# Ten raw weight buffers and five low-part buffers in a two-layer decoder trunk, with another landing time in its planner

## The chip, the cores and the metric

The kernel runs on one core of one Trainium2 chip. The metric is the device time of one execution in microseconds (us); of several executions the median is given. The core has five engines that run side by side, each with its own queue of instructions: TensorE (PE; its weight loads are the row PEld), VectorE (DVE), ScalarE (ACT), GpSimd (POOL) and SyncE (SP), which here issues most of the DMA transfers. Sixteen DMA engines carry the transfers.

## The reference

The kernel computes a decoder trunk of two layers for 256 tokens of width 1024, all in float32. Each layer adds a half-step SwiGLU feed-forward part (FFN, inner width 2816), a mixer, a second FFN and a gated embedding (PLE). The mixer of layer 0 is a chunked mLSTM, that of layer 1 a differential attention over keys and values that are computed once after layer 0.

```python
def swiglu(x, w_in, w_out):
    gate, up = jnp.split(x @ w_in, 2, axis=-1)
    return (jax.nn.silu(gate) * up) @ w_out

for layer in range(DEPTH):                       # DEPTH = 2
    g = norm_g[layer]
    h = swiglu(rms_norm(x, g[0]), w_ffn_in[layer, 0], w_ffn_out[layer, 0])
    x = x + 0.5 * rms_norm(h, g[1])
    h = rms_norm(x, g[2])
    if layer < N_A_LAYERS:                       # layer 0
        h = mlstm_mixer(h, mlstm_w_in[layer], mlstm_b_gates[layer],
                        mlstm_head_norm[layer], mlstm_w_out[layer])
    else:                                        # layer 1
        h = diff_attention(h, k_sh, v_sh, diff_w_q[j], diff_lambda[j],
                           diff_subln[j], diff_w_out[j], lam_init)
    x = x + rms_norm(h, g[3])
    h = swiglu(rms_norm(x, g[4]), w_ffn_in[layer, 1], w_ffn_out[layer, 1])
    x = x + 0.5 * rms_norm(h, g[5])
    gate = jax.nn.sigmoid(rms_norm(x, g[6]) @ w_ple_gate[layer])
    x = x + rms_norm((p[layer] @ w_ple_proj[layer]) * gate, g[7])
    if layer == N_A_LAYERS - 1:
        k_sh, v_sh = shared_kv(x, kv_norm, w_kv)
```

## The kernel before

**Matmuls in three parts.** A float32 product is made of three matmuls of a rounded type (fp32r): each operand is split into a high part and a low part, and high·high, high·low and low·high are added up in PSUM (`mm3`). For activations these are the tiles `xh`/`xl` and `hh`/`hl`, for weights `whi`/`wlo`. Since every weight is used for only 256 tokens, the weights stream through the core once, a piece of 128x2048 (1 MB) at a time.

**The way of a weight piece** (`weight`, line 482, or `load` and `parts` inside `block_pair`): SP issues a transfer into a raw buffer `wraw`; ACT copies it, rounded, to `whi`; DVE subtracts (`wraw` - `whi`) into `wlo`; PE reads `whi` and `wlo`. The raw buffer is free when DVE's subtraction is done, the two parts when PE's last matmul with them is done. In halves (x2, 128x1024) the two copies are made where a stage begins or ends. `part` (line 472) hands out one `whi` and one `wlo`.

**FFN.** The inner width is cut into eleven blocks of 256. Most blocks are taken in pairs (`block_pair`, line 717) with seven products of quarters in place of eight; for that, sums of weight pieces are needed, which DVE adds in place in `wraw`, or POOL makes by a transfer that adds to what a raw buffer holds. `stage_out` multiplies the gated hidden block (`hh`/`hl`, after a transpose on PE into `tr`) with the output weights into four accumulators `accO`. Input products go to `accI`.

**Raw buffers hold other things too.** The residual x (two halves of one buffer, `pair`), the gains of the next norm, the normed x for the pairs (`pre` with `kept`), and the mLSTM's and the attention's values are `wraw` tiles for a time. There are 9 raw buffers, 6 `whi` and 6 `wlo` (128x2048, 8 KB for each partition).

**What sets the order.** The program is run twice. The first run only notes every operation (`Notes.add`); then `play` (line 266) simulates the engines with a table of costs, and takes at each step, greedily, the operation that can start first, in the order of the program among equals. It also hands out the buffers: a tile gets the next slot that comes free, in the order in which tiles are created. The second run issues the operations in the order found (line 432, which is therefore the line of nearly all instructions in the profile). Each engine then runs its instructions strictly in that order, and waits where the buffer or the data isn't there. In the simulation a transfer's data counts as there some time after its bytes are through: 180 ns and `LATE` for a plain transfer, 810 ns and `SLACK` for one that adds (in `later`, inside `play`):

```python
def later(q, t):
    t += 810 + SLACK if q.kw.get("accum_op") is not None else 180 + LATE
```

The names that the prediction uses: `wraw`, `whi_Nr`, `wlo_Nr` (N is the slot), `hh`/`hl`, `tr`, `accI`/`accO`, `att` (pieces of 128x512 for transposed x, attention and held sums), `sg` (gated hidden block).

Of the kernel before, what the change touches and what calls it, by code (L numbers as in the profile page):

```python
# [10 lines left out]
F32R = mybir.dt.float32r  # L11
# [5 lines left out]
P = 128  # L17
# [7 lines left out]
PEN = 30  # L25
MARGIN = 300
SLACK = 3000
LATE = 600
LANES = 8
DEPTH = 2  # L30
HA = 4
# [2 lines left out]
BIG = 2.0 ** 100  # L34
GKV = 8
ATT = 8
NRAW = 9
NPART = 6
NX = 7
NSG = 3  # L40
NH = 3
# [18 lines left out]
class Notes:  # L60
# [205 lines left out]
    def play(self, margin):  # L266
# [60 lines left out]
        def later(q, t):  # L327
            t += 810 + SLACK if q.kw.get("accum_op") is not None else 180 + LATE
            if t > q.end:
                q.end = t  # L330
                for u in q.users:
                    if u.start is None and u.after[q]:
                        u.ready = max(u.ready, t)
                for v in freed.get(q, ()):
                    given[v] = max(given[v], t)
# [99 lines left out]
def trunk(nc, a):  # L435
    def T(shape, tag, bufs, dt=F32):
        return nc.tile("sb", shape, tag, bufs, dt)
# [32 lines left out]
        nc.vector.scalar_tensor_tensor(dst_lo, src, gc, dst_hi.bitcast(F32), op0=ALU.mult, op1=ALU.subtract)  # L470

    def part():
        return T([P, 2048], "whi", NPART, F32R), T([P, 2048], "wlo", NPART, F32R)


    def pair(*shape):
        b = T([P, 2, *shape], "wraw", NRAW)
        return [b[:, i] for i in range(2)]
# [3 lines left out]
    def weight(src, n=1, m=1, between=None):  # L482
        raw = T([P, 2048], "wraw", NRAW)
        hi, lo = part()
        w = 2048 // n
        was, nc.is_urgent = nc.is_urgent, False
        for i in range(n):
            if between and i in between:
                between[i]()
            c = slice(i * w, (i + 1) * w)  # L490
            nc.sync.dma_start(raw[:, c], src[:, c])
            for i2 in range(m):
                c2 = slice(i * w + i2 * w // m, i * w + (i2 + 1) * w // m)
                split(hi[:, c2], lo[:, c2], raw[:, c2])
        nc.is_urgent = was
        return hi, lo
# [28 lines left out]

    xT = T([P, KD, NT, P], "wraw", NRAW)

# [81 lines left out]
    def quarter_parts():  # L609
        return T([P, 4, P], "xh", NX, F32R), T([P, 4, P], "xl", NX, F32R)  # L610

# [43 lines left out]
    def parked(tiles):  # L655
# [4 lines left out]
        def back():  # L660
            b = T([P, 2, D], "wraw", NRAW)
            nc.sync.dma_start(b, home)
            return [b[:, i].rearrange("p (a b) -> p a b", b=v.shape[2]) for i, v in enumerate(tiles)]
# [53 lines left out]
    def block_pair(xts, xf, src, src2, use, end=False, between=None, nxt=None, t3=None):  # L717
        def load(src, plus=None):
            raw = T([P, 2048], "wraw", NRAW)
            nc.sync.dma_start(raw, src)  # L720
            if plus is not None:
                nc.gpsimd.dma_start(raw, plus, accum_op=ALU.add)
            return raw

        def parts(raw):
            p_ = part()
            split(*p_, raw)
            return p_
# [196 lines left out]
    def ple(l, xts, rs, epilogue):  # L925
        gbc, hg = load_gbc(a["norm_g"][l, 7])
        pT = T([P, 2, S], "att", ATT)
        nc.sync.dma_start(pT, a["pT"][l])
        php = T([P, 2, 2, S], "whi", NPART, F32R)
        ph, pl = php[:, 0], php[:, 1]  # L930
# [572 lines left out]
```

## Time and profile before

| | before |
|---|---|
| time, median of 3 runs | 1009.94 us (1007.89 to 1010.15) |
| profiled execution, time | 1006.51 us |
| profiled execution, span | 1004.7 us |
| granted TensorE clock | 0.999 |
| ACT busy | 697.9 us (69%) |
| POOL busy | 88.6 us (9%) |
| DMA | 274.68 MB, mean 273 GB/s |

The trace runs through the stages one after the other, by the weights that SP loads: first FFN of layer 0 from the start (its last weights at 145 us), mLSTM (weights from 149 to 259), second FFN (262 to 436), PLE and the shared keys and values (444 to 485), first FFN of layer 1 (485 to 665), differential attention (667 to 741), last FFN (741 to 930) and the last PLE (937 to the end). The matmuls of a stage come some 10 to 40 us behind its loads. "[3.83 <-DMA wraw]" at the end of a row is the idle time of that engine just before, and what ended it. In the views by windows the counts stand in parentheses. Matmuls overlap, so two rows in succession start 0.23 us apart though one lasts 0.39.

### The profile page before, as it was taken

Reading aid. Unit: us, or ns where it says so; the run is one execution under the profiler, and the core shown is the slowest. Engines: PE = TensorE matmul, PEld = TensorE weight load, DVE = VectorE, ACT = ScalarE, POOL = GpSimd, SP = SyncE. Lnnn points to the kernel's source line nnn. Section 1 sums busy time; section 2 is a strip of 40 time slices with the busy share of each in tenths; the row PEclk is TensorE's granted clock in tenths of the full one; section 3 lists DMA queues with packets and bytes.
Section 4 is the critical chain, followed back from the end, with each engine's and each line's share of the span. In section 5 each row is a group of like instructions: output and inputs, shape, how many; then the busy total and the mean of one; then the engine's idle time right before and its main releaser. Section 6 shows DMA issues by size and latency. Waiting matters only on the chain. (4 is left out here: it accounts for less than half of the span.)

```text
span 1004.7 us, 12418 instructions
## 1 busy us (share of the span) xinstructions
PE 987.2 (98%) x4636; PEld 803.2 (80%) x4636; DVE 893.1 (89%) x909; ACT 697.9 (69%) x924; POOL 88.6 (9%) x126
## 2 busy tenths in 40 slices
PE   9999999999999999999999999999999999999997
PEld 7888888887787788888887788788888887888886
DVE  6977998788999999998899899998985999999983
ACT  8747767577847867595767767676776787767662
POOL 0000000100131000001120000000002300000010
PEclk9999999999999999999999999999999999999999
DMA  9999778765699999966799999965657898998721
GB/s 345 418 333 335 234 245 301 241 191 186 252 292 339 290 337 311 311 252 221 293 280 321 349 335 326 311 248 222 232 216 230 241 330 285 286 306 283 282 84 42
DMA packets 45860, 274.68 MB, mean 273 GB/s; under 512 B 5481, under 2 KB 5865, under 8 KB 16105
## 3 DMA queue, kind: packets, MB, share of 16 engines
q1 hardware_dynamic: 39752, 231.69, 60.1%
q0 software_dynamic: 5760, 41.95, 20.8%
q8 instruction: 36, 0.59, 0.2%
q10 hardware_dynamic: 288, 0.27, 0.1%
q14 instruction: 24, 0.19, 0.0%
HBM read 263.40 MB, written 10.49 MB: 273 GB/s over the span
## 5 line engine op out<-in xcount | busy, mean ns | idle before, releaser
L432 DVE TENSOR_TENSOR wraw<-wraw,wraw 128x2048 f32<-128x2048 f32 x40 | 91.3, 2282 | 0.2
L432 ACT ACTIVATE whi_0r<-wraw 128x2048 fp32r<-128x2048 f32 (+2 forms) x49 | 77.8, 1597 | 11.7 <-DMA wraw<-in_mlstm_in 3.8
L432 ACT ACTIVATE whi_2r<-wraw 128x2048 fp32r<-128x2048 f32 (+1 forms) x48 | 79.4, 1663 | 7.7 <-PE accI L432 3.5
L432 ACT ACTIVATE whi_1r<-wraw 128x2048 fp32r<-128x2048 f32 (+2 forms) x51 | 78.2, 1542 | 7.4 <-PE accO L432 4.1
L432 ACT ACTIVATE whi_5r<-wraw 128x2048 fp32r<-128x2048 f32 (+1 forms) x44 | 71.7, 1641 | 15.6 <-PE accI L432 11.5
L432 ACT ACTIVATE whi_4r<-wraw 128x2048 fp32r<-128x2048 f32 (+1 forms) x45 | 73.7, 1648 | 6.0 <-PE accO L432 2.6
L432 ACT ACTIVATE whi_3r<-wraw 128x2048 fp32r<-128x2048 f32 (+1 forms) x45 | 74.1, 1648 | 4.9 <-DMA wraw<-in_ffn_in 3.3
L432 ACT ACTIVATE att<-accI 128x512 f32<-128x512 f32 x80 | 47.5, 593 | 34.0 <-PE accI L432 33.7
L432 POOL DMA_DIRECT2D wraw<-in_ffn_in x36 | 32.0, 888 | 426.3 <-DMA wraw<-in_ffn_in 363.3
L432 DVE TENSOR_TENSOR wlo_0r<-wraw,whi_2r 128x2048 fp32r<-128x2048 f32 (+1 forms) x25 | 48.3, 1942 | 1.3 <-ACT whi_2r L432 1.3
L432 DVE TENSOR_TENSOR wlo_3r<-wraw,whi_1r 128x2048 fp32r<-128x2048 f32 (+1 forms) x25 | 48.4, 1941 | 1.1 <-ACT whi_1r L432 1.1
L432 DVE TENSOR_TENSOR wlo_2r<-wraw,whi_2r 128x2048 fp32r<-128x2048 f32 (+1 forms) x21 | 43.7, 2080 | 4.6 <-ACT whi_2r L432 4.5
L432 DVE TENSOR_TENSOR wlo_1r<-wraw,whi_1r 128x2048 fp32r<-128x2048 f32 (+2 forms) x26 | 44.4, 1709 | 3.5 <-ACT whi_1r L432 3.4
L432 DVE TENSOR_TENSOR wlo_1r<-wraw,whi_0r 128x2048 fp32r<-128x2048 f32 (+1 forms) x23 | 46.0, 2005 | 0.4 <-ACT whi_0r L432 0.2
L432 DVE TENSOR_TENSOR wlo_0r<-wraw,whi_0r 128x2048 fp32r<-128x2048 f32 (+2 forms) x24 | 44.1, 1839 | 0.8 <-ACT whi_0r L432 0.6
L432 DVE TENSOR_TENSOR wlo_5r<-wraw,whi_4r 128x2048 fp32r<-128x2048 f32 (+1 forms) x23 | 44.0, 1912 | 0.3 <-ACT whi_4r L432 0.3
L432 DVE TENSOR_TENSOR wlo_4r<-wraw,whi_4r 128x2048 fp32r<-128x2048 f32 (+1 forms) x22 | 43.6, 1991 | 0.3 <-ACT whi_4r L432 0.3
L432 POOL TENSOR_TENSOR sm<-sm,mhalf 128x1 f32<-128x1 f32 (+2 forms) x40 | 32.5, 813 | 109.0 <-DVE sm L432 106.5
L432 DVE TENSOR_TENSOR wlo_2r<-wraw,whi_3r 128x2048 fp32r<-128x2048 f32 (+1 forms) x22 | 41.7, 1894 | 0.3 <-ACT whi_3r L432 0.3
L432 DVE TENSOR_TENSOR wlo_4r<-wraw,whi_5r 128x2048 fp32r<-128x2048 f32 (+1 forms) x22 | 41.4, 1894 | 0.0
L432 POOL TENSOR_SCALAR sm<-sm 128x1 f32<-128x1 f32 x32 | 16.9, 527 | 261.8 <-ACT sg L432 261.8
L432 ACT ACTIVATE sg<-accI,sm 128x256 f32<-128x256 f32 x34 | 16.0, 471 | 32.9 <-PE accI L432 24.2
(617 smaller groups left out, 3041.4 us busy)
## 6 DMA issues: line engine op xcount, KB each, us to landing
wraw<-in_ffn_in SPq DMA_DIRECT2D x102, 1024.0 KB, 9.5
wraw<-in_ffn_out SPq DMA_DIRECT2D x44, 1024.0 KB, 9.3
wraw<-in_ffn_in POOLq DMA_DIRECT2D x36, 1024.0 KB, 12.0
wraw<-in_mlstm_in SPq DMA_DIRECT2D x14, 1024.0 KB, 6.9
wraw<-in_ple_gate SPq DMA_DIRECT2D x8, 1024.0 KB, 5.5
wraw<-in_w_kv SPq DMA_DIRECT2D x8, 1024.0 KB, 5.1
home<-wraw SPq DMA_DIRECT2D x28, 256.0 KB, 4.1
wraw<-home SPq DMA_DIRECT2D x14, 512.0 KB, 3.4
```

The costliest lines, as they stand in the source:

```text
L432: getattr(getattr(self.nc, eng), name)(*args, **kw)
```

## The change

One buffer of 8 KB for each partition moves from the low parts to the raw pieces: ten `wraw` and five `wlo` in place of nine and six; `whi` stays at six. The planner takes a plain transfer to land 1000 ns after its bytes are through (beside the 180) in place of 600. The costs of the operations stay, and so does what is computed.

```diff
-LATE = 600
+LATE = 1000
...
-NRAW = 9
+NRAW = 10
 NPART = 6
+NLOW = 5
...
     def part():
-        return T([P, 2048], "whi", NPART, F32R), T([P, 2048], "wlo", NPART, F32R)
+        return T([P, 2048], "whi", NPART, F32R), T([P, 2048], "wlo", NLOW, F32R)
```

Since the planner hands out buffers and picks the order, instructions move on all engines. Three places matter below. In the rows `wraw_3_80` is raw buffer 3; the number behind it only tells tiles of the pools apart and counts differently in the two kernels.

The first place is SP, the loads of the mLSTM's weights. The mLSTM's input weights come in a group of nine and a group of five. Before, these are the last five loads of the first group and the five of the second:

```order
L432 DMA wraw_8_85<-in_mlstm_in 128x2048
L432 DMA wraw_1_78<-in_mlstm_in 128x2048
L432 DMA wraw_0_77<-in_mlstm_in 128x2048
L432 DMA wraw_2_79<-in_mlstm_in 128x2048
L432 DMA wraw_3_80<-in_mlstm_in 128x2048
...
L432 DMA wraw_1_78<-in_mlstm_in 128x2048
L432 DMA wraw_8_85<-in_mlstm_in 128x2048
L432 DMA wraw_3_80<-in_mlstm_in 128x2048
L432 DMA wraw_4_81<-in_mlstm_in 128x2048
L432 DMA wraw_2_79<-in_mlstm_in 128x2048
```

With the change, the same ten loads (left out in both are x going to its home in DRAM and coming back, and two loads of gains):

```order
L433 DMA wraw_2_78<-in_mlstm_in 128x2048
L433 DMA wraw_3_79<-in_mlstm_in 128x2048
L433 DMA wraw_8_84<-in_mlstm_in 128x2048
L433 DMA wraw_6_82<-in_mlstm_in 128x2048
L433 DMA wraw_0_76<-in_mlstm_in 128x2048
...
L433 DMA wraw_8_84<-in_mlstm_in 128x2048
L433 DMA wraw_3_79<-in_mlstm_in 128x2048
L433 DMA wraw_2_78<-in_mlstm_in 128x2048
L433 DMA wraw_0_76<-in_mlstm_in 128x2048
L433 DMA wraw_5_81<-in_mlstm_in 128x2048
```

The third load of the second group, the one at 221.02 us in the trace of before, takes raw buffer 3 before, which the last load of the first group had filled; with the change it takes raw buffer 2, which the first load of the first group had filled, four loads earlier.

The second place is DVE at the end of the differential attention, ahead of the last FFN; `xl_5r<-tr,sub` is a low part of the attention's result, the `sm4` rows are softmax and norm sums. Before (the two halves of the split at 764.68 us in the trace are the third row):

```order
L432 SCALAR_TENSOR_TENSOR xl_5r_118<-tr_0_97,sub_0_164,xh_5r_111 128x512
L432 TENSOR_TENSOR wlo_4r_75<-wraw_0_77,whi_5r_70 128x1024
L432 TENSOR_TENSOR wlo_1r_72<-wraw_4_81,whi_0r_65 128x1024 x2
L432 SCALAR_TENSOR_TENSOR sm4_4_138<-sm4_2_136,sm4_0_134 128x2
L432 TENSOR_TENSOR wraw_7_84<-accO_2_95,sm4_3_137 128x256
L432 SCALAR_TENSOR_TENSOR sm4_9_143<-sm4_8_142,sm4_7_141 128x2
```

With the change, from the same `xl_5r` row on, and then the rows where that piece's split stands now:

```order
L433 SCALAR_TENSOR_TENSOR xl_5r_118<-tr_0_97,sub_0_164,xh_5r_111 128x512
L433 SCALAR_TENSOR_TENSOR sm4_4_138<-sm4_2_136,sm4_0_134 128x2
L433 TENSOR_TENSOR wraw_2_78<-accO_2_95,sm4_3_137 128x256
L433 SCALAR_TENSOR_TENSOR sm4_9_143<-sm4_8_142,sm4_7_141 128x2
...
L433 SCALAR_TENSOR_TENSOR wraw_8_84<-wraw_1_77,sm1_4_160,wraw_8_84 128x512 x2
L433 SCALAR_TENSOR_TENSOR xl_2r_115<-tr_0_97,sub_0_164,xh_2r_108 128x512
L433 TENSOR_TENSOR wlo_2r_73<-wraw_5_81,whi_4r_69 128x1024
L433 TENSOR_TENSOR att_7_105<-tr_0_97,gcol_0_130 128x512
L433 TENSOR_TENSOR att_2_100<-accI_1_91,gcol_0_130 128x512
L433 TENSOR_TENSOR xl_0r_113<-att_7_105,xh_0r_106 128x512
L433 TENSOR_TENSOR xl_4r_117<-att_2_100,xh_4r_110 128x512
L433 TENSOR_TENSOR wlo_2r_73<-wraw_5_81,whi_4r_69 128x1024
```

One split fewer stands ahead of the attention's last sums; the piece whose split was the third row before is split in two halves after x has been updated (the row into `wraw_8_84`), around the first pieces of the next norm, and the splits behind it come one place later each.

The third place is DVE at the first pair of blocks of the FFN that opens layer 1. Before, from the split in halves at 525.22 us on:

```order
L432 TENSOR_TENSOR wlo_4r_75<-wraw_1_78,whi_5r_70 128x1024 x2
L432 TENSOR_TENSOR wlo_3r_74<-wraw_4_81,whi_1r_66 128x2048
L432 COPY wraw_6_83<-tr_0_97 128x4x128
L432 TENSOR_TENSOR xl_5r_118<-att_1_99,xh_5r_111 128x512
L432 TENSOR_TENSOR wraw_4_81<-wraw_4_81,wraw_5_82 128x2048
L432 TENSOR_TENSOR wlo_1r_72<-wraw_3_80,whi_0r_65 128x2048
L432 SCALAR_TENSOR_TENSOR sg_2_128<-accI_1_91,sm1_2_158,sg_2_128 128x256
```

And with the change:

```order
L433 TENSOR_TENSOR wlo_0r_71<-wraw_4_80,whi_1r_66 128x1024
L433 TENSOR_TENSOR xl_5r_118<-att_0_98,xh_5r_111 128x512
L433 TENSOR_TENSOR wlo_0r_71<-wraw_4_80,whi_1r_66 128x1024
L433 COPY wraw_9_85<-tr_0_97 128x4x128
L433 TENSOR_TENSOR wlo_4r_75<-wraw_3_79,whi_2r_67 128x2048
L433 TENSOR_TENSOR wlo_3r_74<-wraw_2_78,whi_4r_69 128x2048
L433 SCALAR_TENSOR_TENSOR sg_0_126<-accI_0_90,sm1_2_158,sg_0_126 128x256
L433 TENSOR_TENSOR wraw_3_79<-wraw_3_79,wraw_8_84 128x2048
```

The two whole splits (128x2048) of the pair's first pieces now follow each other, and the add in place (`wraw<-wraw,wraw`), which stood between them, follows the gating row.

## The prediction, made before the result was known

> **What bounds the kernel now.** I read the head of the page, then the busy time in pieces of 20 us, then the waits of SP, then the timelines of the pieces that fall behind.
>
> ```profile
> span 1004.7 us, 12418 instructions
> PE 987.2 (98%) x4636; PEld 803.2 (80%) x4636; DVE 893.1 (89%) x909; ACT 697.9 (69%) x924; POOL 88.6 (9%) x126
> ```
>
> PE looks busy throughout, but matmuls overlap, so its row hides pauses. Weight loads (PEld) show them better. The columns below are the piece, its length, then busy time (count) of PE, PEld, DVE, ACT and POOL, the clock, the DMA share, GB/s.
>
> ```profile
> 220.00:240.00 20.00, 19.50 (x89) 15.03 (x88) 16.10 (x26) 14.47 (x20) 0.86 (x1) 1.00 0.82 245
> 240.00:260.00 20.00, 19.50 (x92) 15.63 (x91) 18.85 (x26) 18.08 (x32) 3.01 (x1) 1.00 0.42 156
> 300.00:360.00 60.00, 57.67 (x257) 45.38 (x256) 57.86 (x55) 45.72 (x52) 5.78 (x7) 1.00 0.99 327
> 380.00:400.00 20.00, 20.00 (x92) 16.31 (x91) 19.89 (x16) 13.82 (x14) 0.88 (x1) 1.00 1.01 344
> 640.00:660.00 20.00, 19.01 (x86) 14.99 (x85) 17.61 (x16) 11.01 (x12) 0.00 (x0) 1.00 0.73 256
> 840.00:860.00 20.00, 18.48 (x80) 13.76 (x79) 19.10 (x15) 10.30 (x12) 0.86 (x1) 1.00 1.00 348
> ```
>
> The piece at 380 is a full one: 92 matmuls and 16.31 us of loads in 20.00, or 0.816 of the time. Time that PE loses elsewhere is (16.31 of each 20 us, less the loads) / 0.816: 1.57 at 220, 0.83 at 240, 4.4 over 300 to 360, 1.62 at 640, 3.13 at 840. The other pieces lack less each (260, quoted below, as much as 640), so these places hold most of what an order or a buffer can win: 11.6 us of 1004.7.
>
> [...] By PE's row the places above would hold about 6 us, by the loads about twice that; the terms below rest on single stalls instead.
>
> What sets a weight load's time is its buffer:
>
> ```profile
> SPq L432 <- DVE wraw L432: 143.3, 48, 17.1
> SPq L432 <- DVE wlo_1r L432: 111.1, 25, 16.1
> ```
>
> SP waits for DVE to be done with a raw buffer (total, times, longest); a raw buffer is held from the load's issue until DVE has written the low part. So **a tenth raw buffer lets a load be issued one release earlier**, and one low buffer less makes DVE write a low part only when PE is done with the one five back, not six.
>
> **Part 1, the load that mLSTM's end waits for: -2.0.**
>
> ```profile
> 210.99 2.29 DVE L432 TENSOR_TENSOR wlo_2r<-wraw,whi_2r 128x2048 fp32r<-128x2048 f32 x1 [0.28 <-ACT whi_2r L432]
> 218.68 2.27 DVE L432 TENSOR_TENSOR wlo_3r<-wraw,whi_3r 128x2048 fp32r<-128x2048 f32 x1
> 221.02 0.33 SPq L432 DMA_DIRECT2D wraw<-in_mlstm_in  x1
> 233.10 1.92 ACT L432 ACTIVATE whi_0r<-wraw 128x2048 fp32r<-128x2048 f32 x1 [3.83 <-DMA wraw<-in_mlstm_in]
> 235.53 0.69 DVE L432 TENSOR_TENSOR att<-att,att 128x512 f32<-128x512 f32 x1 [3.76 <-ACT att L432]
> ```
>
> The load at 221.02 waits for the split that ends at 218.68 + 2.27 = 220.95. It lands at 233.10; ACT stands for it 3.83 us with the attention work queued behind it, and DVE stands 3.76 behind ACT. In the new order (the first place of the section on the change) this load takes a buffer filled four loads earlier, whose split is the row at 210.99: free at 213.28, or 7.67 us earlier. That exceeds 3.83, even if half is lost in the queue (share 0.82 here). PE loses 1.57 + 0.83 = 2.4 at 220 to 260. Ends: 0 (the head of the next chain is late anyway) and -2.4. I take -2.0: DVE then runs ahead by its 3.76, which is more than the lost 2.4, but some of 240 to 260 lies in mLSTM's own chain of small steps.
>
> **Part 2, the same in the two long FFNs: -1.2 and -0.6.**
>
> ```profile
> 628.08 2.28 DVE L432 TENSOR_TENSOR wlo_2r<-wraw,whi_3r 128x2048 fp32r<-128x2048 f32 x1
> 635.62 2.28 DVE L432 TENSOR_TENSOR wraw<-wraw,wraw 128x2048 f32<-128x2048 f32 x1
> 637.93 0.33 SPq L432 DMA_DIRECT2D wraw<-in_ffn_in  x1
> 648.80 1.92 ACT L432 ACTIVATE whi_3r<-wraw 128x2048 fp32r<-128x2048 f32 x1 [2.14 <-DMA wraw<-in_ffn_in]
> 651.01 0.42 DVE L432 TENSOR_TENSOR hl_2r<-tr,hh_1r 128x256 fp32r<-128x256 f32 x1 [1.64 <-ACT hh_1r L432]
> 651.49 0.44 PE L432 MATMUL tr<-ident,sg 128*128 128x128 f32 x2 [0.99 <-DVE hl_2r L432]
> ```
>
> The load at 637.93 goes out when the add at 635.62 ends (637.90). ACT stands 2.14 for it, ACT's copy hh_1r and DVE's hl_2r come behind it, and PE stands 0.99 for that (1.15 by the matmuls' starts). One release earlier is the split that ends at 628.08 + 2.28 = 630.36: 7.5 us sooner, against 2.14 needed. I take -1.2, with ends 0 and -1.62 (the piece's whole loss).
>
> ```profile
> 820.68 2.29 DVE L432 TENSOR_TENSOR wlo_1r<-wraw,whi_0r 128x2048 fp32r<-128x2048 f32 x1
> 835.68 0.33 SPq L432 DMA_DIRECT2D wraw<-in_ffn_in  x1
> 846.26 1.92 ACT L432 ACTIVATE whi_3r<-wraw 128x2048 fp32r<-128x2048 f32 x1 [0.55 <-DMA wraw<-in_ffn_in]
> 850.68 0.50 PE L432 MATMUL accO<-wlo_5r,hh_1r 128*128 128x512 f32 x1 [1.15 <-DVE wlo_5r L432]
> ```
>
> At 835.68 the earlier release is 820.68 + 2.29 = 822.97, 12.7 us sooner, but ACT waits only 0.55 for this load, and PE's stall of 1.15 is for DVE, which works 19.10 of 20 us here. I take about the 0.55: -0.6, ends 0 and -3.13 (whole piece).
>
> **Part 3, DVE's lead carried on: -1.0.** Over 300 to 360 PE loses 4.4 us where DVE is busy 57.86 of 60.00. DVE's 3.76 idle at 235 becomes lead if its work up to 300 has data early; but the chain of the next norm holds it up (DVE 18.39 of 20 at 260, below), and what it does in advance needs free low buffers. Ends 0 and -3.76; I take the lower third, -1.0, since the piece at 260 shows DVE waiting again.
>
> ```profile
> 260.00:280.00 20.00, 18.71 (x95) 14.99 (x94) 18.39 (x29) 14.84 (x18) 1.92 (x1) 1.00 0.69 256
> ```
>
> **Part 4, one low part fewer: +1.0.** In a stage where PE has plenty prepared, DVE would wait:
>
> ```profile
> 175.14 2.29 DVE L432 TENSOR_TENSOR wlo_3r<-wraw,whi_3r 128x2048 fp32r<-128x2048 f32 x1
> 180.51 0.61 PE L432 MATMUL accO<-wlo_4r,hh_2r 128*128 128x512 f32 x2
> 194.89 0.40 PE L432 MATMUL accI<-wlo_3r,xh_2r 128*128 128x512 f32 x1
> ```
>
> The fifth buffer back is last read at 180.51 + 0.61 = 181.12, so this write moves 5.98 us; its first use at 194.89 leaves 17.45 us, hence 11.5 remain: nothing is lost. Where DVE is the bound, little is prepared, so the fifth buffer is free in time: at 640.42 DVE writes a low part, and the one five back is read last at 638.30.
>
> ```profile
> 638.30 0.39 PE L432 MATMUL accI<-wlo_1r,xh_3r 128*128 128x512 f32 x1
> 640.42 2.28 DVE L432 TENSOR_TENSOR wlo_3r<-wraw,whi_1r 128x2048 fp32r<-128x2048 f32 x1
> ```
>
> The price falls where one regime meets the other, before the last FFN:
>
> ```profile
> 764.68 2.50 DVE L432 TENSOR_TENSOR wlo_1r<-wraw,whi_0r 128x1024 fp32r<-128x1024 f32 x2
> 781.97 0.62 PE L432 MATMUL accO<-wlo_2r,xh_3r 128*128 128x512 f32 x2
> 764.00:784.00 20.00, 20.00 (x117) 17.09 (x115) 9.10 (x17) 10.13 (x30) 4.58 (x7) 1.00 1.01 302
> 784.00:812.00 28.00, 28.00 (x135) 23.09 (x133) 27.36 (x32) 22.17 (x33) 8.22 (x8) 1.00 0.85 242
> 810.17 2.28 DVE L432 TENSOR_TENSOR wlo_3r<-wraw,whi_1r 128x2048 fp32r<-128x2048 f32 x1
> 812.68 0.40 PE L432 MATMUL accI<-wlo_3r,xh_2r 128*128 128x512 f32 x1
> ```
>
> The split at 764.68 (2.50 us) lies in a stretch where DVE works 9.10 of 20.00 us. With five buffers it must wait for the reading that ends at 781.97 + 0.62 = 782.59; the new order (second place) has it behind the norm. From 784 to 812 DVE works 27.36 of 28.00, so 0.64 is free, and at 812.68 PE uses a low part that was ready at 812.45, 0.23 before. Of 2.50, up to 2.50 - 0.64 - 0.23 = 1.6 then reaches PE, if nothing else in the stretch gives way. The stalls of Part 2 at 840 come after it, and a delayed PE has its later low parts more in advance. I take +1.0; ends 0 and +2.5. At the entry to the first FFN of the second layer a split of the same kind moves too (2.4 us, two halves of 1.22):
>
> ```profile
> 485.40 1.22 DVE L432 TENSOR_TENSOR wlo_3r<-wraw,whi_1r 128x1024 fp32r<-128x1024 f32 x1
> 533.09 2.28 DVE L432 TENSOR_TENSOR wlo_1r<-wraw,whi_0r 128x2048 fp32r<-128x2048 f32 x1
> 535.58 0.40 PE L432 MATMUL accI<-wlo_1r,xh_1r 128*128 128x512 f32 x1
> ```
>
> There the part used at 535.58 was ready 0.21 before, but the new order (third place) puts its split ahead of an add of 2.28 us that stood before it; the two cancel, 0 (ends 0 and +2.4).
>
> **LATE** changes only the order: it lets the plan assume 400 ns more for a plain load. Alone it moves few rows that wait, so it has no term; its ends are the -0.6 and +0.6 of a wait such as the 0.55 at 846.26.
>
> **Sum:** -2.0 - 1.2 - 0.6 - 1.0 + 1.0 = -3.8 on the profiled execution's 1006.51, or 1002.7. The median of the runs shown is 1009.94, 3.43 above this execution; the same change on it gives **1006.1**.
>
> **Rivals.**
>
> *The entries cost DVE in full (slower).* The low parts that move from idle stretches, 2.4 us at 485 and 2.5 at 764, all reach PE, because DVE has only 0.64 us free up to the first use 0.23 later, and Parts 1 to 3 give only -1.0 together. +4.9 - 1.0 = +3.9: **1013.8**. It decides when DVE's free time between the norm and 812 is under the 2.50 moved in. For it: 27.36 of 28.00. Against: the order at 535.58 turns the other way, and ACT and DVE wait on landing at both ends.
>
> *An earlier issue lands no earlier (same).* Where the 16 DMA engines are full (share 0.99 over 300 to 360, 1.00 at 840), a load issued earlier only stands longer behind the ones before it. Then only Part 1's load, with share 0.82 and 0.42, gains: -2.0 + 1.0 = -1.0, **1008.9**. For it: those shares. Against: 0.73 at 640. [...]
>
> *DVE's lead is kept (faster by more).* Part 3 at its end: -3.76 in place of -1.0, so -6.6: **1003.4**. Against: the wait at 260.
>
> *The change does nothing*, since LATE is not what the chip does and DVE is the bound: 1009.9.
>
> **How the numbers follow.** The forecast 40%, the entries in full 17%, no earlier landing 22% and nothing 9%, the lead kept 12%. About 0.3% (3.0 us) is what a measurement of this kernel can tell from no change, so 1006.9 to 1012.9 is the same. Of the forecast's 40%, 7 points lie above 1006.9: faster .33 + .12 = .45, same .07 + .22 + .09 = .38, slower .17. The range runs from 1000.5 (the lead kept and Part 2's ends) to 1013.0 (most of the slower rival left out); about 2 in 10 lie outside.
>
> **What would show it.** Right: ACT no longer waits 3.83 for a load near 233, the loads at 220 to 260 rise to about 32.6 together, and ACT's 2.14 before hh_1r near 649 goes. Part 4: DVE busier past 784, with a new stall of PE for a low part between 800 and 840. Wrong: the same waits on landing at a later place, or loads that stay out longer than now, when the three above took 12.1, 10.9 and 10.6 us from issue to the ACT copy.

## The result, and the profile after

| | before | after |
|---|---|---|
| median of 5 runs | 1009.52 us (1007.67 to 1010.15) | 1003.42 us (1003.14 to 1004.18) |
| ratio, 95% interval | | 0.9942 (0.9928 to 0.9956) |
| profiled execution | 1006.51 us, span 1004.7 | 1004.18 us, span 1002.4 |

The change makes the kernel 6.1 us faster where 3.8 were forecast. The two profiled executions, though, differ by only 2.3 us. So there are two questions: where the 2.3 come from, and where the other 3.8 are.

The head of the page after, and the pieces that were read before (length, then busy time of PE, PEld, DVE, ACT and POOL, the clock, the DMA share, GB/s):

```profile
span 1002.4 us, 12436 instructions
PE 988.7 (99%) x4636; PEld 801.8 (80%) x4636; DVE 893.2 (89%) x909; ACT 700.8 (70%) x926; POOL 96.7 (10%) x126
...
220.00:240.00 20.00, 20.00 (x92) 15.50 (x90) 18.94 (x29) 16.95 (x22) 0.00 (x0) 1.00 0.72 204
240.00:260.00 20.00, 19.60 (x94) 16.01 (x92) 18.70 (x24) 17.76 (x26) 3.02 (x1) 1.00 0.57 211
260.00:280.00 20.00, 20.00 (x102) 16.45 (x102) 19.25 (x31) 12.60 (x22) 1.94 (x3) 1.00 0.77 294
300.00:360.00 60.00, 58.41 (x260) 45.69 (x260) 59.66 (x56) 45.24 (x52) 5.26 (x7) 1.00 1.00 336
640.00:660.00 20.00, 20.00 (x93) 16.40 (x93) 19.46 (x17) 14.43 (x15) 0.00 (x0) 1.00 0.70 267
784.00:812.00 28.00, 27.27 (x125) 21.51 (x124) 27.01 (x30) 20.28 (x27) 7.49 (x6) 1.00 0.90 266
800.00:820.00 20.00, 18.86 (x83) 14.52 (x81) 19.97 (x19) 14.45 (x17) 0.95 (x1) 1.00 0.93 296
840.00:860.00 20.00, 19.70 (x86) 15.24 (x85) 19.39 (x16) 13.92 (x14) 0.86 (x1) 1.00 0.96 317
```

The weight loads rise at 220, 240, 640 and 840, where the prediction looked for it: 30.66 to 31.51 from 220 to 260, 14.99 to 16.40 at 640, 13.76 to 15.24 at 840; and at 260, from 14.99 to 16.45. A new gap stands at 800, 14.52 against the 16.29 that the trace of before has there:

```profile
800.00:820.00 20.00, 20.00 (x96) 16.29 (x95) 19.27 (x24) 19.06 (x25) 1.58 (x3) 1.00 0.92 298
```

Since both kernels run the same matmuls on the same data, each one can be matched. The table gives its start in the kernel that the column names less its start in the first profile of before, in us, as the median over the matmuls of 20 us of before's trace from the place named on. The other columns are experiments that follow below, and the second and third profile of before. Between 240 and 280 the new orders move matmuls against one another, by up to 18 us later and 5 us earlier, so the row at 240 tells little there of how far PE is ahead; the readings go by 220 and 280.

| place | after | low part alone | nine in mLSTM | ten in mLSTM only | before, 2nd profile | before, 3rd profile |
|---|---|---|---|---|---|---|
| 220 | +0.5 | +1.1 | +0.3 | +0.4 | +0.5 | -0.3 |
| 240 | -2.6 | +2.3 | -0.5 | -2.6 | +1.2 | +2.5 |
| 280 | -2.3 | +4.8 | +1.9 | -2.3 | +1.2 | +2.3 |
| 320 | -0.8 | +4.8 | +2.0 | -0.6 | +1.2 | +2.3 |
| 340 | -3.8 | +6.3 | +1.9 | -0.5 | +2.8 | +2.3 |
| 360 | -3.1 | +6.3 | +1.7 | +0.9 | +2.8 | +2.3 |
| 420 | -2.2 | +6.4 | +2.5 | +3.0 | +2.8 | +2.3 |
| 520 | -1.6 | +6.5 | +3.0 | +3.4 | +2.9 | +2.8 |
| 560 | -3.0 | +5.0 | +1.7 | +1.9 | +2.9 | +2.9 |
| 620 | -3.2 | +6.8 | +1.4 | +3.8 | +2.9 | +2.8 |
| 640 | -4.5 | +6.4 | +0.2 | +3.3 | +2.9 | +2.8 |
| 800 | -4.0 | +5.3 | +0.6 | +2.5 | +3.2 | +2.7 |
| 820 | -1.7 | +5.3 | +2.9 | +2.5 | +3.2 | +2.7 |
| 860 | -2.8 | +5.0 | +1.8 | +3.8 | +3.2 | +2.9 |
| 980 | -2.0 | +5.4 | +2.6 | +4.3 | +3.3 | +3.0 |

So the schedule gains 2.8 by mLSTM's end (from +0.5 at 220 to -2.3 at 280), 0.8 by 360, 1.4 between 520 and 560, 1.3 at 640 and 1.1 near 850, and gives back 1.5 from 360 to 520, 0.5 from 640 to 800, 2.3 at 800 and 0.8 after 860. The 1.4 at 520 to 560 come with the low part alone as well (+6.5 to +5.0), which has nine raw buffers, so they belong to the new order and not to the tenth buffer. The same caution holds at 640: both columns with nine raw buffers there fall too, from +6.8 to +5.3 and from +3.8 to +2.5 between 620 and 800. That the tenth buffer makes the gain at 640 is therefore not shown.

The load that mLSTM's end waited for, in the timeline of after:

```profile
214.40 0.33 SPq L433 DMA_DIRECT2D wraw<-in_mlstm_in  x1
...
225.41 1.91 ACT L433 ACTIVATE whi_0r<-wraw 128x2048 fp32r<-128x2048 f32 x1
232.95 1.92 ACT L433 ACTIVATE whi_1r<-wraw 128x2048 fp32r<-128x2048 f32 x1 [2.32 <-DMA wraw<-in_mlstm_in]
...
235.38 0.69 DVE L433 TENSOR_TENSOR att<-att,att 128x512 f32<-128x512 f32 x1 [0.92 <-ACT att L433]
```

It goes out at 214.40 in place of 221.02, and ACT copies it at 225.41 without a wait (before: 233.10 after 3.83). ACT now waits 2.32 for the load behind it, but DVE stands only 0.92 of its 3.76, and PE not at all. At 640 the piece that ACT waited for until 648.80 goes out at 630.32 in place of 637.93 and is copied without a wait:

```profile
630.32 0.33 SPq L433 DMA_DIRECT2D wraw<-in_ffn_in  x1
...
642.29 1.90 ACT L433 ACTIVATE whi_0r<-wraw 128x2048 fp32r<-128x2048 f32 x1
```

### The profile page after: what moved, and what is told of

It reads as the page before. It is cut to its first block, busy times and chain, and to the rows that moved or that the text cites. A ratio compares the mean times of both kernels' runs of the same rounds, so it can differ in the third digit from the quotient of the medians.

```text
span 1002.4 us, 12436 instructions
## 1 busy us (share of the span) xinstructions
PE 988.7 (99%) x4636; PEld 801.8 (80%) x4636; DVE 893.2 (89%) x909; ACT 700.8 (70%) x926; POOL 96.7 (10%) x126
## 4 chain that ended last, share of the span: by engine, by line
PE 78%; DVE 6%; ACT 5%; issue 4%; DMA 4%; POOL 2%; SPq 0%; DVEq 0%; POOLq 0%; ACTq 0%
PE accI L433 47%; PE accO L433 28%; PE tr L433 4%; POOL sm L433 2%; ACT sg L433 1%; DMA wraw<-in_ffn_in 1%; DMA wraw<-in_mlstm_in 1%; DVE wlo_4r L433 1%; DVE att L433 1%; DVE wraw L433 1%; DVE wlo_1r L433 1%; DMA wraw<-in_x 1%; DVE wlo_0r L433 1%; DMA wraw<-in_xT 1%; ACT att L433 1%
## 5 line engine op out<-in xcount | busy, mean ns | idle before, releaser
L433 ACT ACTIVATE sg<-accO 128x512 bf16<-128x512 f32 (+2 forms) x46 | 20.2, 444 | 24.5 <-PE accO L433 21.9
L433 ACT ACTIVATE sg<-att,sm 128x256 f32<-128x256 f32 x54 | 26.7, 503 | 14.1 <-DVE att L433 13.7
L433 PEld LDWEIGHTS tr<-ident,sg 128*128 128x128 f32 x176 | 22.0, 140 | 17.1 <-DVE hl_1r L433 3.9
L433 PE MATMUL tr<-ident,sg 128*128 128x128 f32 x176 | 34.7, 279 | 0.2 <-DVE hl_0r L433 0.2
L433 DVE SCALAR_TENSOR_TENSOR wraw<-wraw,sm,wraw 128x512 f32<-128x512 f32 x32 | 22.7, 749 | 12.7 <-POOL sm L433 12.7
L433 DVE TENSOR_TENSOR att<-accI,att 128x512 f32<-128x512 f32 x40 | 27.4, 684 | 2.7 <-PE accI L433 2.4
L433 ACT ACTIVATE sg<-wraw 128x512 bf16<-128x512 f32 x32 | 20.2, 630 | 12.9 <-DVE wraw L433 11.5
L433 ACT ACTIVATE att<-accI,sm 128x512 f32<-128x512 f32 (+1 forms) x22 | 14.8, 671 | 18.6 <-PE accI L433 18.5
L433 ACT ACTIVATE hh_2r<-tr 128x256 fp32r<-128x256 f32 x28 | 10.6, 378 | 23.4 <-PE accO L433 14.9
L433 DVE SCALAR_TENSOR_TENSOR sg<-att,sm,sg 128x256 f32<-128x256 f32 x54 | 25.6, 479 | 1.6 <-ACT sg L433 1.3
## 6 DMA issues: line engine op xcount, KB each, us to landing
wraw<-in_ffn_in POOLq DMA_DIRECT2D x36, 1024.0 KB, 12.1
```

The source lines that it names most:

```text
L433: getattr(getattr(self.nc, eng), name)(*args, **kw)
```

## The experiments

### Which part of the change counts

**LATE alone**, **the buffers alone**, **the low part given up for nothing**, and **a high part given up in place of the low one**:

```diff
 # LATE alone, against before          # buffers alone, against after
-LATE = 600                            -LATE = 1000
+LATE = 1000                           +LATE = 600
 # low part alone, against after       # high part given up, against after
-NRAW = 10                             -  "whi", NPART ... "wlo", NLOW
+NRAW = 9                              +  "whi", NLOW ... "wlo", NPART
```

(With the high part given up, a `whi` tile of the PLE takes `NLOW` as well.)

> Nine raw buffers, six low parts, LATE 1000. Theory (the tenth raw buffer makes the gain, LATE has no term): 1009.5 +-1.5, and ACT's wait of about 3.8 us for the mLSTM load near 233 stays. Rival (the planner's landing time makes the gain by a better order): about 1003.5 to 1005.

> Ten raw buffers, five low parts, LATE 600. Theory: 1003.4 +-1.5, as with the whole change. Rival (LATE makes the gain): about 1009. Rival (any new order moves the time by some us, whatever the buffers): anywhere between 1000 and 1010.

> Nine raw buffers, five low parts, LATE 1000: the low part is given up and nothing is got for it. Theory: the price of the low part without the gain, 1010.5 to 1014 (the last FFN's entry cost PE about 2.4 us in the changed kernel), with the wait of 3.8 us at the mLSTM's load back. Rival (five low parts cost nothing, and the 2.4 us there come from the new order of the pairs): 1009.5 +-1.

> Ten raw buffers, five high and six low parts, LATE 1000: the tenth raw buffer paid for with a high part. Theory (a high part is held longer than its low part, from ACT's copy on, so it is dearer; ACT, ahead of DVE, is held up): 1004 to 1008, with the mLSTM's wait gone. Rival (parts are in plenty, either can go): 1003.4 +-1. Rival (a high part bounds the chain ACT, DVE, PE everywhere): over 1010.

| | median us (runs) | ratio to before, 95% |
|---|---|---|
| before, same chip | 1009.72 (23) | |
| LATE alone | 1009.80 (12) | 1.0007 (0.9995 to 1.0020) |
| buffers alone | 1004.26 (6) | 0.9947 (0.9930 to 0.9963) |
| low part alone | 1010.84 (12) | 1.0005 (0.9990 to 1.0021) |
| high part given up | 1019.94 (6) | 1.0101 (1.0083 to 1.0119) |

The exchange of buffers makes the gain and LATE has none. With nine raw buffers throughout ACT's wait at mLSTM's end is back; the row is that of the kernel with the low part alone:

```profile
235.33 1.91 ACT L433 ACTIVATE whi_0r<-wraw 128x2048 fp32r<-128x2048 f32 x1 [4.94 <-DMA wraw<-in_mlstm_in]
```

Giving up a low part costs nothing that can be measured: 1.0005 against 1.0007 for LATE alone, which has six. Its median, 1010.84, lies at the lower end of the expected 1010.5 to 1014, but its twelve runs go from 1007.08 to 1012.56, so the expected cost of 1 to 4.5 us isn't shown. A high part is another matter: it is claimed earlier, by ACT's copy, and with five of them the kernel is 10 us slower, over the theory's 1004 to 1008 and as the last rival had it. What makes the 10 us was not taken apart; the longest of PE's waits for a single operand there is one for ACT's copy into a high part:

```profile
845.43 0.65 PE L433 MATMUL accI<-whi_4r,xh_2r 128*128 128x512 f32 x1 [2.18 <-ACT whi_4r L433]
```

### Where the tenth raw buffer is needed

One raw buffer is held empty in a part of the program. The code shows the first of two runs; in the second the two calls stand around the first FFN, and again from the mLSTM's end to the end of the last FFN:

```diff
+    def hold():
+        b = T([P, 2048], "wraw", NRAW)
+        nc.gpsimd.memset(b[:, 0:1], 0.0)
+        return b
+    def let_go(b):
+        nc.gpsimd.tensor_tensor(small(), b[:, 0:1], x[0][:, 0:1], op=ALU.add)
...
+    b = hold()
     xts = mlstm(0, xts, rq, kept, pre(2, rs, xfs=xfs))
+    let_go(b)
```

> The changed kernel with one of the ten raw buffers held empty from the mLSTM's first load to x after its first half. Theory (the tenth buffer gains the 3.0 us at mLSTM's end): PE at 245 us stands 0 to +1 us against before in place of -3.0, ACT's wait of about 4 us for the load comes back, and the later places keep their gains: 1004.5 to 1008.5. Rival (the order, not the buffer): -3.0 at 245 stays and the time is 1003.4 +-1.

> The changed kernel with one raw buffer held empty before the mLSTM and from its end to the end of the last FFN: ten in the mLSTM, nine elsewhere, five low parts. Theory: PE at 245 at about -3 against before, no gain at 640 and 850: 1006.5 +-1.5. Rival (the tenth buffer is worth its most in the FFNs, where raw buffers are waited for 143 us in all): 1009 to 1011.

Nine in the mLSTM: 1010.73 us (12 runs), 1.0001 (0.9987 to 1.0015). Ten in the mLSTM only: 1009.50 us (12 runs), 1.0002 (0.9990 to 1.0014). **Either half alone gives back the whole gain.** For the second the rival's range holds; the first lies above both of its ranges. The table of starts shows how. With ten in the mLSTM only, the gain of the mLSTM is there in full (+0.4 at 220, -2.3 at 280), and gone by 420: from 280 to 420 PE falls back 5.3 us. There DVE, with nine raw buffers, stands idle for ACT:

```profile
353.90 0.48 DVE L433 SCALAR_TENSOR_TENSOR sg<-att,sm,sg 128x256 f32<-128x256 f32 x1 [2.46 <-ACT sg L433]
...
388.84 0.88 DVE L433 SCALAR_TENSOR_TENSOR sg<-att,sm,sg 128x256 f32<-128x256 f32 x2 [1.92 <-ACT sg L433]
```

With ten, DVE works 59.66 of 60.00 us from 300 to 360, and the lead is kept. With nine in the mLSTM, the later gains stay (another 1.2 between 620 and 640), but PE has fallen back to +1.9 by 280. It isn't the load's wait that came back: the load goes out late, at 221.28, and yet ACT waits only 0.76 for it where about 4 were expected. The loss comes behind it, in two pauses of PE for DVE, and the piece of 260 to 280 shows a lower clock:

```profile
230.29 1.92 ACT L433 ACTIVATE whi_0r<-wraw 128x2048 fp32r<-128x2048 f32 x1 [0.76 <-DMA wraw<-in_mlstm_in]
...
268.00 0.66 PE L433 MATMUL tr<-ident,wraw 128*128 128x128 f32 x4 [1.08 <-DVE wraw L433]
270.81 0.50 PE L433 MATMUL accI<-wlo_3r,xh_4r 128*128 128x512 f32 x1 [2.14 <-DVE wlo_3r L433]
...
260.00:280.00 20.00, 16.77 (x70) 13.19 (x69) 18.16 (x29) 14.37 (x17) 1.92 (x1) 0.91 0.79 303
```

The same pair of pauses (1.1 and 2.14 us) stands in LATE alone and in the low part alone, near 270, but not in before, which has nine raw buffers and LATE 600. All three plan with LATE 1000 and nine buffers there, so it belongs to that order, and not to a late load. Every change of the buffers changes the order too, and no run here holds the order still: what the tenth buffer gains by the load alone is not separated from what it gains by the order.

The lower clock was the lead to the missing 3.8 us.

### The clock behind a pause

The kernel before was profiled twice more, and the changed one once more.

> The kernel before, unchanged, another profiled execution. Between the two first profiles the spans differ by 2.3 us, the medians by 6.1. Theory (the rest is TensorE's clock: where PE pauses for over about 2 us, the granted clock is 0.5 for some 3.5 us after, as at 274 us in the run with LATE alone; in the first profile of before no pause did it, in most of its executions one to three do): a span of 1006 to 1010 with one to three pieces of 20 us at about 0.91, each behind a pause of PE at 270, 340, 650 or 849, and each worth 1.7 us. Rival (loads land later in most executions than in the first profile): the clock is 1.00 throughout and the span is over 1006 all the same.

> The same again; as for the first look. By the theory the number of pieces below 0.95 orders the spans of the three profiles of before, at about 1.7 us for each.

> The changed kernel, unchanged, a second profiled execution. Clock theory (the changed kernel has no pause of PE long enough): no piece of 20 us under 0.99 between 20 and 980 us, span 1001.5 to 1003. Rival (the first profile of the changed kernel had luck, as the first of before): a piece near 0.91 and a span near 1004.

| execution | span, us | pieces of 20 us below 0.99 from 20 to 980 us |
|---|---|---|
| before, first profile | 1004.7 | none |
| before, second profile | 1008.0 | 0.91 at 340 |
| before, third profile | 1007.7 | 0.94 at 220, 0.97 at 240 (one stretch across both) |
| after, first profile | 1002.4 | none |
| after, second profile | 1001.7 | none |

The first profile of before was its fast end. The spans do stand in the order of the drops of the clock (none, one, one), but 3.0 to 3.3 us apart, where 1.7 for each was expected: the second thing that differs is the rival's, a load that lands later. In the second profile, PE's two waits near 342 are the same as in the first, but here the clock goes to half behind them (pieces of 2 us):

```profile
341.91 0.50 PE L432 MATMUL accI<-whi_1r,xh_1r 128*128 128x512 f32 x1 [1.14 <-ACT whi_1r L432]
343.30 0.50 PE L432 MATMUL accI<-wlo_4r,xh_2r 128*128 128x512 f32 x1 [0.89 <-DVE wlo_4r L432]
...
342.00:344.00 2.00, 1.11 (x4) 0.71 (x5) 2.00 (x3) 2.00 (x3) 0.00 (x0) 0.99 0.23 82
344.00:346.00 2.00, 2.00 (x7) 1.52 (x6) 2.00 (x2) 0.14 (x1) 0.87 (x1) 0.50 0.78 246
346.00:348.00 2.00, 2.00 (x8) 1.58 (x7) 2.00 (x2) 0.29 (x1) 0.00 (x0) 0.66 1.13 315
```

And the first profile of before, at the same waits:

```profile
340.69 0.50 PE L432 MATMUL accI<-whi_1r,xh_1r 128*128 128x512 f32 x1 [1.14 <-ACT whi_1r L432]
342.08 0.50 PE L432 MATMUL accI<-wlo_4r,xh_2r 128*128 128x512 f32 x1 [0.89 <-DVE wlo_4r L432]
...
344.00:346.00 2.00, 2.00 (x10) 1.63 (x10) 2.00 (x2) 1.05 (x2) 0.87 (x1) 1.00 0.90 369
```

Seven matmuls in 2 us in place of ten. The two pieces at 0.50 and 0.66 have lost (0.50 + 0.34) x 2 = 1.7 us, and the column of the second profile jumps by 1.6 there. In the third profile ACT copies the load at mLSTM's end 1.3 us later than in the first (at 234.38, with a wait of 5.43), PE pauses for 2.10 where it paused for 0.50, and the clock drops behind it:

```profile
236.83 0.50 PE L432 MATMUL accI<-whi_4r,xh_4r 128*128 128x512 f32 x1 [2.10 <-ACT att L432]
...
220.00:240.00 20.00, 17.90 (x78) 13.95 (x77) 14.51 (x24) 13.61 (x18) 0.61 (x1) 0.94 0.82 242
240.00:260.00 20.00, 19.60 (x91) 15.75 (x90) 17.99 (x26) 17.27 (x31) 3.01 (x1) 0.97 0.33 109
```

That is a coincidence seen several times, not yet a cause. So four pauses were put into the changed kernel, in its first FFN, where PE is the bound (`last` is what the matmul before wrote, `w` a small tile):

```diff
+            if i in PAUSES:          # ahead of four products' first matmul
+                nc.scalar.activation(w[:, 4:5], last[:, 0:1], AF.Copy)
+                for n in (4, 5, 4, 5):
+                    nc.gpsimd.tensor_scalar(w[:, 9 - n:10 - n], w[:, n:n + 1], w[:, 7:8], None, op0=ALU.add)
+                nc.tensor.matmul(args[0][:, 0:1], ident, w[:, 4:5], start=True, stop=True)
```

> The changed kernel with four pauses of PE put into the first FFN near 41, 58, 75 and 89 us, where low parts lie ready for 9 us and more: ACT reads one column of the product that has just ended, POOL copies it four times (0.53 us each), and one small matmul of PE reads the last copy and holds the next product up. By the rows of those operations a pause is 2.6 to 3.4 us. Clock theory (a pause of over about 2 us is followed by a granted clock of 0.5 for some 3.5 us): pieces of 20 us at about 0.91 behind most of the four, each worth 1.7 us beside the pause itself, so 1003.4 + 10.4 to 13.6 for the pauses + 3.4 to 6.8 for the clock = 1017 to 1024. Rival (the drops that other runs show have another cause and only fall beside pauses): clock 1.00 throughout, 1013.8 to 1017. A pause that is made up later (rival of both) would give under 1013.

1024.09 us (4 runs), 20.7 above the changed kernel and at the upper end of the clock theory's range. The four pauses, and the pieces of 4 us behind the second and the third:

```profile
44.87 0.59 PE L442 MATMUL accI<-mhalf,ident 128*128 128x1 f32 x2 [3.43 <-POOL mhalf L441]
66.84 0.38 PE L442 MATMUL accI<-mhalf,ident 128*128 128x1 f32 x2 [1.83 <-POOL mhalf L441]
87.62 0.38 PE L442 MATMUL accI<-mhalf,ident 128*128 128x1 f32 x2 [1.83 <-POOL mhalf L441]
107.31 0.38 PE L442 MATMUL accI<-mhalf,ident 128*128 128x1 f32 x2 [3.50 <-POOL mhalf L441]
...
64.00:68.00 4.00, 2.17 (x11) 1.54 (x10) 0.48 (x1) 0.54 (x2) 1.13 (x4) 0.99 1.00 268
68.00:72.00 4.00, 4.00 (x14) 3.09 (x13) 0.71 (x2) 0.39 (x2) 0.09 (x1) 0.58 1.00 414
...
84.00:88.00 4.00, 2.17 (x11) 1.51 (x11) 1.03 (x2) 0.54 (x2) 1.23 (x5) 1.00 0.00 0
88.00:92.00 4.00, 4.00 (x13) 3.14 (x13) 0.37 (x1) 0.38 (x1) 0.80 (x1) 0.57 0.71 123
```

Each of the four is followed by a drop. The pauses sum to 10.6 us; the pieces of 20 us from 40 on stand at 0.83, 0.91, 0.91 and 0.91. The second and the third drop took 0.42 x 4 and 0.43 x 4, or 1.7 us each; the first lasted twice as long, which stays open. At 3.4 for it and 1.7 for the others the clock takes 8.5 us. Together 19.1, against 19.8 between the spans (1022.2 and 1002.4). The rival without a clock (at most 1017) is out: **two pauses of PE of 1.83 us were each followed by the slow clock, which cost 1.7 us more.** The "over about 2 us" of the expectations was the author's estimate from LATE alone, where the clock stood at 0.50 from 274 to 276 us behind pauses of 1.1 and 2.14.

The length of a pause alone doesn't tell whether a drop follows. The two waits near 342 are 1.14 and 0.89 us in the first profile of before and in the second; from 344 to 346 the clock stood at 1.00 in the first and at 0.50 in the second. What makes the difference is not shown. Nor is it shown whether the pauses of 1.83 us would be followed by a drop in other executions, since only one with them was traced.

### The loss before the last FFN

In the changed kernel PE waits at 809.70 for a low part, 0.69 us:

```profile
804.17 2.28 DVE L433 TENSOR_TENSOR wraw<-wraw,wraw 128x2048 f32<-128x2048 f32 x1
...
807.36 2.29 DVE L433 TENSOR_TENSOR wlo_4r<-wraw,whi_3r 128x2048 fp32r<-128x2048 f32 x1
...
809.70 0.50 PE L433 MATMUL accI<-wlo_4r,xh_5r 128*128 128x512 f32 x1 [0.69 <-DVE wlo_4r L433]
```

In the kernel with ten raw buffers in the mLSTM only, DVE makes that add before it updates x, and PE loses nothing there. So the add was moved forward, in the last FFN, and then in both FFNs that follow a mixer (of what DVE can start, the planner takes what is marked `is_urgent` first):

```diff
+        nc.is_urgent = early         # l == 1 and f == 1 and n == 0; then f == 1 and n == 0
         w21 = parts(b21)
...
             nc.vector.tensor_tensor(out, v0, v1, op=ALU.add)
+            nc.is_urgent = False
             return parts(out)
```

> The changed kernel with DVE's split of the second piece and the add behind it (wraw<-wraw,wraw, at 804.17 in its profile) marked urgent in the first pair of the last FFN alone, so that they stand ahead of the update of x. Theory (PE's loss of 2.35 us from 800 to 820 comes from that add, which the ten-buffer order puts behind the next norm's pieces, not from the low part that moved): the loss goes to 0 to 0.5, 1001.0 to 1002.3. Rival (the 2.5 us of the moved split are DVE work that has to be done there in any order): 1003.4 +-0.7, with the loss at another place between 800 and 850.

> The same mark in the first pair of both FFNs that follow a mixer; the FFN after the mLSTM shows the same picture near 309 us (the add at 309.05, PE waits 0.64 at 314.58 and 0.47 at 318.43). Theory: a further 0.8 to 1.3 us at 300 to 320, 1000.0 to 1001.5. Rival (DVE works 59.66 of 60 us from 300 to 360, so what is won at 314 is lost by 360): as the run with the last FFN alone, +-0.5.

1005.16 us (5 runs), 0.9962 (0.9948 to 0.9975), and 1008.36 us (11 runs), 0.9989 (0.9979 to 0.9998): both slower than the change as it stands, by 1.7 and 4.9 us (for the first the interval overlaps with the change's own, 0.9928 to 0.9956). The theory fell, and the first lies above its rival's range (1002.7 to 1004.1) too. By the matched starts the first wins 0.7 us by 820 against the changed kernel and is 1.1 behind at 860; DVE works 26.96 of 28.00 us from 784 on, against 27.01, so here the other order only moved the loss. The second loses 4.9 us between 320 and 340 against the changed kernel, and its piece at 340 has a clock of 0.91. The buffers are those of the changed kernel, so a few operations in other places are enough to cost most of its gain. The low part that moved isn't the cause by itself either: with five low parts and nine raw buffers the same split comes as late (its two halves, below), and PE loses nothing from 800 to 820 (+5.3 and +5.3 in the table).

```profile
789.43 1.22 DVE L433 TENSOR_TENSOR wlo_0r<-wraw,whi_4r 128x1024 fp32r<-128x1024 f32 x1
...
793.16 1.22 DVE L433 TENSOR_TENSOR wlo_0r<-wraw,whi_4r 128x1024 fp32r<-128x1024 f32 x1
```

What makes the 2.3 us there stays open: it comes with the ten-buffer order (the kernel with nine in the mLSTM has it too, +0.6 to +2.9), not with five low parts as such.

## Why the prediction was right, and where it was off

**The bound and the mechanism** held in the main: raw buffers set the issue of loads, the tenth lets loads out earlier, and the loads at 220 to 260 rose, to 31.51 where 32.6 was named as full. LATE counts for nothing in all, as said.

**Part 1 (-2.0)** measured -2.8 by 280. The load went out 6.6 us earlier, not 7.7, and ACT copied it 7.7 us earlier. It even exceeds the 2.4 that were taken as its end, since that end was read from 220 to 260 alone and the piece at 260 filled up too. What of it is the load's and what the order's isn't separated: with nine in the mLSTM the load's wait was short as well (0.76), and the time was lost just behind it. With ten in the mLSTM only, the whole of it is lost again by 420 (-2.3 to +3.0).

**Part 2 (-1.2 and -0.6)** measured -1.3 and -1.1. The load near 638 did go out earlier, but two kernels with nine raw buffers there gain as much from 620 to 800, so the tenth buffer as the cause of the first term isn't shown; the second was almost twice its price. The rival that an earlier issue lands no earlier fell: ACT copied the piece of 637.93 at 642.29, not 648.80. On the whole, though, loads stayed out a little longer (the FFN's input pieces 9.9 us from issue to landing against 9.5).

**Part 3 (-1.0)** measured -0.8 between 280 and 360, as a loss of 1.5 by 320 and a gain of 3.0 at 340, with 0.7 back by 360. That the net came near its price is partly luck, since only a gain was forecast; and its weight wasn't seen. That DVE can keep the lead is what the gain at mLSTM's end depends on, and it takes the tenth buffer in the FFN as well.

**Part 4 (+1.0, ends 0 and +2.5)** is the step whose mechanism failed. A loss of 2.3 came at the place that was named, and yet five low parts alone cost nothing that shows, there or in all. The price was put on the moved split; it belongs to the order that comes with ten buffers. DVE wasn't busier from 784 to 812 either (27.01 against 27.36), only from 800 to 820 (19.97 against 19.27). At the entry of the other FFN nothing was lost beyond 0.3, as said.

**The sum** on the profiled executions, -2.3, is 1.5 short of the forecast's -3.8; Part 4 alone is 1.3 of it. **The step that missed the size was the last one**: "the median of the runs shown is 1009.94, 3.43 above this execution; the same change on it". Those 3.43 us were no constant. The changed kernel's median lies 0.76 below its first profiled execution, so this step was 4.2 us off one way and the sum 1.5 the other; that the forecast came within 2.7 is in part luck. So is it that the rival "DVE's lead is kept" named the measured 1003.4: its mechanism, Part 3 at -3.76, isn't what the trace shows (-0.8).

What the 3.43 us are can be told in part. The second and third profile of before are typical executions (1009.77 and 1009.50, where the median of 23 others is 1009.40), and so is the second of after (1003.43). Their spans are 6.3 and 6.0 apart, which is the whole difference of the medians. Against the first profile of before the two stand 3.3 and 3.0 us later. In each, one drop of the clock is 1.7 of it. Another 0.7 and 1.6 are the load at mLSTM's end, which took 12.8 and 13.7 us from issue to ACT's copy in place of 12.1, so that PE waited 1.21 and 2.10 us behind it in place of 0.50. The changed kernel has neither: PE doesn't wait there, and its longest wait between 21 and 980 us in the first profile is the 0.69 at 809.70, where the first profile of before had 1.14 and 0.89 (340), 0.99 (651) and 1.15 (850). Neither of the changed kernel's two profiles has a piece of 20 us below 0.99 from 20 to 980.

Over many executions the clock is the smaller part of it. A mean clock of 0.999 excludes a drop of the 1.7 us measured above, which would be 0.0017 of 1009 us. Of the 68 executions of before that ran beside the experiments, 14 have that clock, and their median is 1008.67: 2.2 us above the first profile without any drop. What varies in those was not traced.

## What to carry to other kernels

A profile is one execution: when it lies several us below the median, look at the granted clock and at PE's pauses before taking the gap as fixed, and profile once more. Here pauses of TensorE of 1.83 and 2.10 us among dense matmuls were each followed by a slow clock that cost 1.7 us beside their own length, and so was a pair of 1.14 and 0.89 us in one profile and not in another; so shortening the few longest pauses can be worth more than their sum. A buffer that takes a stage's wait away pays only if the next stage can keep the lead. And where a planner makes a new order with each buffer, the gain of a buffer and that of the order come together.

## What was not expected of the hardware

The same pauses of PE, 1.14 and 0.89 us near 342, were followed by a clock of 0.50 (344 to 346 us) in one execution of before and of 1.00 in another. In the kernel with four pauses the two of 1.83 us were followed by pieces of 4 us at 0.58 and 0.57. The load at mLSTM's end took 12.1, 12.8 and 13.7 us in three executions of one program, and the program's time went from 1006.64 to 1012.80 us over 23 runs; with both the wait for that load and the pauses gone it went from 1003.14 to 1004.18 us, over 5 runs, where the first 5 of before went from 1007.67 to 1010.15.
